# Weight sums of the recurrence stage: adding transfers in one spaced list that is held while a head is normalised, copies in 256 KB pieces on the load queue

## The chip, the cores and the metric

The kernel runs on one core of a Trainium2 chip. The metric is the device time of one execution in microseconds, the median of several runs; lower is better. The core has a matrix engine (TensorE, in the profile PE, with its weight loads as PEld), a vector engine (DVE), a scalar engine (ACT), GpSimd (POOL), and SyncE (SP), which only issues transfers. Each engine works through its own instructions in the order in which the program writes them, and waits where an instruction needs something that another engine or a transfer has yet to deliver. Transfers (DMAs) are issued by SP (the load queue, queue 1 in the profile) and by POOL (queue 0); both are carried out by the same 16 DMA engines.

## What is computed

A decoder of two layers works on 1024 tokens of width 1024 in float32. The first layer's token mixer is a gated linear recurrence with 8 heads, the second's a causal convolution module; each is followed by a squared-ReLU feed-forward part of width 4096, with normalisation after every part. What matters here is the first mixer, cut to its core:

```python
proj = h @ w_in                                   # q | forget | value | output gate
q = silu(q); f = lb + (1 - lb) * sigmoid(fz); k = 1 - f
o = chunkwise_gated_recurrence(q, k, v, cumsum(log f))          # per head
o = o * rsqrt(mean(o * o, axis=-1) + 1e-6) * norm_g             # per head
out = (o * silu(g)) @ w_out
...
ff = square(relu(x @ ffn_w1[i])) @ ffn_w2[i]      # i = 0, 1
```

The line with `rsqrt` is the normalisation of a head.

## The kernel before

All large products are in float32 accuracy: each operand is split into a high and a low part, and a product takes three matmuls. The products of 2x2 blocks are done with seven block products instead of eight (the forms 1, 2, 6, 5, 7, 3, 4 in `ORDER`), for which sums of weight blocks are needed. For `ffn_w2`, which is used from about 870 us on, these sums are not made on the compute engines. They are made by transfers from DRAM to DRAM in advance: `block_sums` (line 399) makes, for one of 16 blocks of `ffn_w2` (two layers by eight), four sums of 512 KB each in a DRAM tensor `sum_w`. For one block it issues:

- two copies of 1 MB each, `v[:, 0:2]` and `v[:, 2:4]` (lines 419 and 420),
- an adding transfer of 1 MB onto `v[:, 0:2]` (line 421), which needs the first copy,
- two adding transfers of 512 KB (line 423), `v[:, 2] += v[:, 1]` and `v[:, 3] += v[:, 2]`, each of which needs the one before.

Adding transfers can be issued by POOL alone. In the recurrence stage the copies go through POOL as well. Twelve of the sixteen blocks are summed in this stage, the other four later in the program, in other ways.

The recurrence stage (about 60 to 420 us) is written out by hand in order. Its outer loop goes over 12 `PAIRS` of weight columns (line 1007), and for each over the 7 forms. `pair_product` issues 12 matmuls of 512 columns for one form, in four slots of three; after each slot `slot` calls `tick` (line 390), which advances a counter and issues the jobs that `later(n, job)` has put off to this tick. So the tick is the unit in which the order of all engines is written. Ticks say nothing of when an instruction runs: an engine that waits for nothing runs ahead of the written order.

Between the products the heads' recurrences are advanced by `step`, one part of the generator `recurrence` (line 634) at a time. The last parts of a head are these: `outer`, then `attend` for the first half of the tokens and, one tick later, `settle(0)`; then `attend` for the second half and, one tick later, `settle(1)`. `settle` (line 731) has ACT square the head's output and sum it (line 735), POOL make the scale with a TENSOR_SCALAR (line 736) and a power of -1/2 (line 518, in `power_m_half`) on a tile `ss`, and ACT apply the scale to `o` (line 741, four ticks later). `give` (line 746) then has PE transpose `o`; ACT writes the result to `kt` (line 754), and SP stores it to DRAM as `od` (line 762).

POOL has hardly more to do in this stage than `settle`'s two instructions and the transfers of `block_sums`. `block_sums` is called after every sixth form, with `gap=12`: the first copy at once, the second 6 ticks later, the three adding transfers 12, 24 and 36 ticks after the call.

SP issues, in written order, the weight blocks `pr` (line 585, 256 KB, a new one as soon as a buffer of five is free), the heads' values `v` (line 632), the heads' stores `od` (line 762), their loads `u` (line 916) and the gated stores `zd` (line 924).

Of the kernel before, what the change touches and what calls it, by code (L numbers as in the profile page):

```python
# [12 lines left out]
ALU = mybir.AluOpType  # L13
PSUM = bass.MemoryType.PSUM

P = 128
# [18 lines left out]
NPAR = TAP + KB * TAPS  # L35

KBYTES = 220
PAIRS = [("q", 0), ("q", 1), ("q", 2), ("q", 3), ("g", 0), ("q", 4), ("q", 5), ("q", 6), ("g", 1), ("q", 7), ("g", 2), ("g", 3)]
NPOOL = (12, 11)
SEQ = "P00 P01 P02 P03 P04 P05 P06 P07 P10 P11 P12 P13 N0 P14 F0 P15 S0 P16 P17 UA0 UA1 E2 E3 N1 E4 F1 E5 E6 S1 E7 UB0 UB1 L2 L3 L4 L5 L6 L7"  # L40
# [4 lines left out]
ORDER = (1, 2, 6, 5, 7, 3, 4)  # L45
# [223 lines left out]
def body(ctx, tc, d, out):  # L269
    nc = tc.nc  # L270
    cst = ctx.enter_context(tc.tile_pool(name="cst", bufs=1))
    stat = ctx.enter_context(tc.tile_pool(name="stat", bufs=4))
    dram = ctx.enter_context(tc.tile_pool(name="dram", bufs=1, space=bass.MemoryType.DRAM))
    space = ctx.enter_context(tc.tile_pool(name="space", bufs=1)).ring(KBYTES * 1024)
    banks = ctx.enter_context(tc.tile_pool(name="ps", bufs=1, space=PSUM)).tile([P, 8, HT], F32, name="ps")
# [4 lines left out]
    def view(kb, shape, dt=F32, name="t"):  # L280
        at, top = int(kb * 1024), KBYTES * 1024
        if at < edge[0]:
            if edge[0] < top:
                space.tile([P, (top - edge[0]) // 4], F32, name="gap")
            edge[0] = 0
        if at > edge[0]:
            space.tile([P, (at - edge[0]) // 4], F32, name="gap")
        edge[0] = at + (prod(shape) + 7) // 8 * 32
        return space.tile([P, *shape], dt, name=name)
# [90 lines left out]
    vd = [[dram.tile([P, NTB, HT], F32, name=f"vd{m}{n}") for n in range(2)] for m in range(2)]  # L380

    ticks, waiting = [0], []

    def later(n, job):
        if n:
            waiting.append((ticks[0] + n, job))
        else:
            job()

    def tick(n=1):  # L390
        for _ in range(n):
            ticks[0] += 1
            for at, job in [w for w in waiting if w[0] <= ticks[0]]:
                waiting.remove((at, job))
                job()

    sums = {}

    def block_sums(name, layer, c, after=None, gap=0, adds=None):

        t = sums[name, layer, c] = dram.tile([4, P, 1024], F32, name=f"sum_{name}{layer}{c}")
        v, w = t.rearrange("a p n -> p a n"), d[name][layer, c].rearrange("a p n -> p a n")
        queue = nc.sync if after is not None else nc.gpsimd
        if adds is not None:

            def copies(rows, after):
                nc.sync.dma_start(out=t[0:4:2, rows.start, 0:1], in_=after)
                queue.dma_start(out=v[rows, 0:2], in_=w[rows, 0:4:2])
                queue.dma_start(out=v[rows, 2:4], in_=w[rows, 0:2])

            copies(slice(16, P), after)
            adds.append(lambda after: copies(slice(0, 16), after))
            adds.append(lambda after: nc.gpsimd.dma_start(out=v[:, 0:2], in_=w[:, 2:4], accum_op=ALU.add))
            for i in (2, 3):
                adds.append(lambda after, i=i: nc.gpsimd.dma_start(out=v[:, i], in_=v[:, i - 1], accum_op=ALU.add, max_dma_last_dim=4096))
            return
        if after is not None:
            nc.sync.dma_start(out=t[0:4:2, 0, 0:1], in_=after)
        queue.dma_start(out=v[:, 0:2], in_=w[:, 0:4:2])
        later(gap // 2, lambda: queue.dma_start(out=v[:, 2:4], in_=w[:, 0:2]))  # L420
        parts = [lambda: nc.gpsimd.dma_start(out=v[:, 0:2], in_=w[:, 2:4], accum_op=ALU.add)]
        for i in (2, 3):
            parts.append(lambda i=i: nc.gpsimd.dma_start(out=v[:, i], in_=v[:, i - 1], accum_op=ALU.add, max_dma_last_dim=4096))
        for i, part in enumerate(parts):
            later((i + 1) * gap, part)

    to_sum = [(*of, c) for of in (("w2", 0), ("w2", 1)) for c in range(NFC)]

# [72 lines left out]
    for k in range(4):  # L501
        c = slice((k % 2) * HT, (k % 2 + 1) * HT)
# [14 lines left out]
    def power_m_half(dst, src, n):  # L517
        nc.gpsimd.tensor_tensor(out=dst, in0=src, in1=nhalf[:, :n], op=ALU.pow)  # L518
# [61 lines left out]
    def load_block():  # L580
        p, b = divmod(at_block[0], 4)
        if p < len(PAIRS) and free:
            at_block[0] += 1
# [3 lines left out]
    def make_form(wait=1):  # L587
        p, i = divmod(at_form[0], 7)
        if p == len(PAIRS):
            return  # L590
# [30 lines left out]
    qk, gates, vts = {}, {}, {}  # L621
# [12 lines left out]
    def recurrence(h):  # L634
# [71 lines left out]
        for n in (32, 64):  # L706
            for s in range(0, n2, 2 * n):
                c, r = divmod(s, P)
# [22 lines left out]
        def settle(half):  # L731
            ss = stat.tile([P, 2, 4], F32, tag="ss", name="ss")
            cs = range(half * NTB, half * NTB + NTB)
            for c in cs:
                nc.scalar.activation(o[:, c], out_ps[:, c, :], AF.Square, scale=1.0 / QSCALE, accum_out=ss[:, 0, c % NTB : c % NTB + 1])
            nc.gpsimd.tensor_scalar(out=ss[:, 1], in0=ss[:, 0], scalar1=1.0 / P, scalar2=RMS_EPS, op0=ALU.mult, op1=ALU.add)
            power_m_half(ss[:, 0], ss[:, 1], 4)

            def rest():
                for c in cs:  # L740
                    nc.scalar.activation(o[:, c], out_ps[:, c, :], AF.Copy, scale=ss[:, 0, c % NTB : c % NTB + 1])
                later(1, lambda: ready.add(half))

            later(4, rest)
# [22 lines left out]
        def values(c):  # L767
            return vts[2 * h + c // NTB][:, c % NTB]

        def outer(cs):  # L770
            for c in cs:
                tensor.matmul(state_ps[:, c % NTB], kt[:, c, :], values(c), start=True, stop=True)

        def chain(cs):
            for c in cs:
                new = p1("state")
                if c == 0:
                    vector.tensor_copy(out=new, in_=state_ps[:, 0])
                else:
                    vector.scalar_tensor_tensor(out=new, in0=states[c], scalar=dec[:, c : c + 1], in1=state_ps[:, c % NTB], op0=ALU.mult, op1=ALU.add)  # L780
                states.append(new)

        def attend(cs):
            for c in cs:
                tensor.matmul(out_ps[:, c, :], A[:, c, :], values(c), start=True, stop=c == 0)
                if c:
                    tensor.matmul(out_ps[:, c, :], Q[:, c * P : (c + 1) * P], states[c], start=False, stop=True)

        outer(range(NTB))
        later(1, lambda: chain(range(NTB)))  # L790
        yield
# [2 lines left out]
        later(1, lambda: (chain(range(NTB, nk)), settle(0)))  # L794
        yield
        attend(range(NTB, 2 * NTB))
        later(1, lambda: settle(1))
        if h < H - 2:
            for half in range(2):
                load_values(2 * h + 2 + half)  # L800
# [23 lines left out]
    def evacuate(p, i, st, ps):  # L824
        kind, j = PAIRS[p]
        m, n = {2: (0, 0), 7: (1, 1), 3: (0, 1)}.get(i, (1, 0))
# [44 lines left out]
    def pair_product(p, i, f, st):  # L871
        ps = banks[:, st["banks"]["a" if i == 2 else "b" if i in (5, 3) else "z"]]
        for k in range(4):
# [5 lines left out]
            if k == 3:  # L879
                later(1 if p == len(PAIRS) - 1 and i in (3, 4) else 3, lambda: evacuate(p, i, st, ps))  # L880
            slot()
# [20 lines left out]
    def slot():  # L902
        tick()
        gate_turn()
        pace[0] += pace[1]
        if pace[0] >= 1:
            pace[0] = pace[0] - 1 if step() else 0.0

    to_load, loaded, to_gate = [], [], []
# [73 lines left out]
    for _ in range(5):  # L983
# [5 lines left out]
    p1 = Room(  # L989
        ((144, 152), (164, 172), (136, 144), (172, KBYTES)),  # L990
        {
# [14 lines left out]
    tick(4)  # L1006
    for p, (kind, j) in enumerate(PAIRS):
        st = {"banks": dict(turn_of)}
        turn_of = {"z": turn_of["a"], "a": turn_of["b"], "b": turn_of["z"]}
        pace[1] = 0.0 if p == 0 else 0.6 if p < 3 else 0.5  # L1010
        if kind == "g" and p < len(PAIRS) - 1:
            to_load += [(2 * j, 0), (2 * j + 1, 1), (2 * j, 1), (2 * j + 1, 0)]
        if p == len(PAIRS) - 1:
            seam()
        for i in ORDER:
            if kind == "q" and i == 2:
                while any(a[0] <= j - 3 for a in active) or recs and recs[0] <= j - 3:
                    tick()
                    step()
            pair_product(p, i, made.pop(0), st)  # L1020
            later(2, make_form)
            if (7 * p + ORDER.index(i)) % 6 == 1 and len(to_sum) > 4:
                block_sums(*to_sum.pop(0), gap=12)
        if kind == "q":
            later(4, lambda j=j: recs.append(j))
    early_out = ((0, 0), (1, 0), (2, 0))
# [7 lines left out]
    while step():  # L1034
        tick()
    tick(100)
    assert not waiting and not loaded and not to_load and not gates, (waiting, gates)
    order.close()
    oT = [o[0] for o in oT]

# [145 lines left out]
    class Up:  # L1186
# [14 lines left out]
        def settle(self, c):  # L1201

            for q in range(2):
                self.first(self.of[c], q)
# [415 lines left out]
    rest, adds = [None, None], []  # L1620
# [303 lines left out]
```

## Time and profile before

| | |
|---|---|
| Median of 3 runs | 2055.2 us (2055.06 to 2062.24) |
| Span of the profiled execution | 2068.3 us (the profile gives no other time of it) |
| PE busy | 2031.0 us, 98% |
| DVE, ACT, POOL busy | 1482.9, 1090.2 and 388.4 us |
| Load queue (queue 1) | 456.93 MB, 62.6% of the 16 engines' span |
| POOL's queue (queue 0) | 58.72 MB, 12.3% |
| Recurrence stage, 60 to 420 us | PE busy 344.72 of 360 us, DMA share 0.89 |

A row of the waits reads: engine, tile and line that waited, what it waited for, then total microseconds, times, and the longest. A row of the timeline reads: start and duration in microseconds, engine, line, operation, what it writes and reads, and in brackets the idle time of the engine before it with what ended that. Matmuls and small vector operations all bear line 204, the line of a helper, and are told apart by their tiles: `ps<-xf,fs` are the products of the recurrence stage, `ps<-ident,o` the transposes of a head's output, `ps` a bank of PE's accumulators, `fs` a weight form and `t` a product on its way to a gate. `sum_w<-in_w_dram` are the copies and the first adding transfer, `sum_w<-sum_w` the other two. POOL's DMA rows show the time for issuing, not for the transfer. A row of the windows gives the stretch and its length, the busy time (and count) of PE, PEld, DVE, ACT and POOL, the granted clock of PE, the DMA share and GB/s.

### The profile page before, as it was taken

Reading aid. Unit: us, or ns where it says so; the run is one execution under the profiler, and the core shown is the slowest. Engines: PE = TensorE matmul, PEld = TensorE weight load, DVE = VectorE, ACT = ScalarE, POOL = GpSimd, SP = SyncE. Lnnn points to the kernel's source line nnn. Section 1 sums busy time; section 2 is a strip of 40 time slices with the busy share of each in tenths; the row PEclk is TensorE's granted clock in tenths of the full one; section 3 lists DMA queues with packets and bytes.
Section 4 is the critical chain, followed back from the end, with each engine's and each line's share of the span. In section 5 each row is a group of like instructions: output and inputs, shape, how many; then the busy total and the mean of one; then the engine's idle time right before and its main releaser. Section 6 shows DMA issues by size and latency. Waiting matters only on the chain. (4 is left out here: it accounts for less than half of the span.)

```text
span 2068.3 us, 29719 instructions
## 1 busy us (share of the span) xinstructions
PE 2031.0 (98%) x11192; PEld 1674.5 (81%) x11192; DVE 1482.9 (72%) x1976; ACT 1090.2 (53%) x1727; POOL 388.4 (19%) x387
## 2 busy tenths in 40 slices
PE   8999999999999999999999999999999999999998
PEld 7888777788888888888888888888878878888886
DVE  8698877877775666565567898889589666755556
ACT  5456555641464555444444776488625555343333
POOL 0112222111001000000001699079210000100002
PEclk9999999999999999999999999999999999999999
DMA  4778889852689786999998855587759778996542
GB/s 186 224 195 233 238 224 270 254 189 81 187 288 298 243 295 221 353 341 332 335 349 292 309 193 185 190 323 271 256 215 339 245 232 291 386 292 204 193 155 102
DMA packets 183944, 517.55 MB, mean 250 GB/s; under 512 B 17912, under 2 KB 49784, under 8 KB 182776
## 3 DMA queue, kind: packets, MB, share of 16 engines
q1 hardware_dynamic: 168312, 456.93, 62.6%
q0 software_dynamic: 15488, 58.72, 12.3%
q8 instruction: 87, 1.43, 0.3%
q14 instruction: 57, 0.47, 0.1%
HBM read 380.85 MB, written 201.85 MB: 282 GB/s over the span
## 5 line engine op out<-in xcount | busy, mean ns | idle before, releaser
L204 PE MATMUL ps<-dw,dh 128*128 128x512 f32 x2688 | 611.6, 389 | 1.9 <-ACT dh L72 1.1
L204 PEld LDWEIGHTS ps<-dw,dh 128*128 128x128 f32 x2688 | 504.1, 188 | 107.2 <-ACT dh L72 1.6
L204 PE MATMUL ps<-x1f,fw 128*128 128x512 f32 x1344 | 309.3, 390 | 2.3 <-DVE c L204 1.2
L204 PEld LDWEIGHTS ps<-x1f,fw 128*128 128x128 f32 x1344 | 251.1, 188 | 56.2 <-ACT c L1224 2.3
L204 PE MATMUL ps<-xf,fs 128*128 128x512 f32 x1008 | 249.3, 398 | 4.1 <-issue 1.9
L204 POOL TENSOR_TENSOR cb<-cb,prod 128x512 f32<-128x512 f32 x168 | 222.7, 1334 | 12.9 <-ACT prod L1555 2.3
L204 DVE TENSOR_TENSOR dh<-dh 128x1024 fp32r<-128x1024 f32 x112 | 136.4, 1222 | 117.3 <-ACT dh L72 117.1
L204 PEld LDWEIGHTS ps<-xf,fs 128*128 128x128 f32 x1008 | 184.5, 189 | 43.4 <-issue 2.1
L204 DVE SCALAR_TENSOR_TENSOR ps<-u,par,ps 128x512 f32<-128x512 f32 x296 | 206.2, 750 | 11.0 <-ACT ps L1567 9.5
L72 ACT CAST dh<-dh 128x1024 fp32r<-128x1024 f32 x112 | 117.4, 1051 | 163.7 <-DMA dh<-hf 163.7
L204 PE MATMUL ps<-xa,wa 128*128 128x512 f32 x864 | 203.1, 392 | 0.1
L204 PEld LDWEIGHTS ps<-xa,wa 128*128 128x128 f32 x864 | 160.3, 188 | 33.3 <-ACT ha L1289 0.3
L204 DVE TENSOR_TENSOR dw<-dr,dw 128x1024 fp32r<-128x1024 f32 x112 | 136.2, 1222 | 66.6 <-ACT dw L72 65.9
L72 ACT CAST dw<-dr 128x1024 fp32r<-128x1024 f32 x112 | 117.0, 1051 | 119.2 <-PE ps L204 100.2
L1555 ACT ACTIVATE prod<-u,par 128x512 f32<-128x512 f32 x168 | 119.8, 726 | 36.6 <-POOL cb L204 35.7
L518 POOL TENSOR_TENSOR mv<-mv,nhalf 128x1 f32<-128x1 f32 x32 | 43.3, 1355 | 407.6 <-DVE mv L204 407.6
L1408 POOL COPY next<-ss 128x1 f32<-128x1 f32 x38 | 21.2, 558 | 413.8 <-DVE spare L204 265.1
L204 PE MATMUL ps<-xb,wa 128*128 128x512 f32 x384 | 91.1, 393 | 0.0
L204 PE MATMUL ps<-w,oT 128*128 128x512 f32 x384 | 89.5, 391 | 1.3 <-ACT oT L932 0.8
L204 DVE TENSOR_TENSOR spare<-next,spare 128x1024 fp32r<-128x1024 f32 x38 | 46.5, 1224 | 60.6 <-ACT spare L1401 60.5
L204 PE MATMUL ps<-vw,xf 128*128 128x512 f32 x336 | 79.8, 399 | 6.0 <-ACT vw L435 5.2
L204 PEld LDWEIGHTS ps<-w,oT 128*128 128x128 f32 x384 | 71.5, 188 | 16.6 <-ACT oT L932 1.2
(236 smaller groups left out, 2959.6 us busy)
## 6 DMA issues: line engine op xcount, KB each, us to landing
wa<-ready SPq DMA_DIRECT2D x140, 512.0 KB, 5.5
dh<-hf SPq DMA_DIRECT2D x112, 512.0 KB, 5.3
sum_w<-in_w_dram POOLq DMA_DIRECT2D x40, 1024.0 KB, 10.9
ready<-spare SPq DMA_DIRECT2D x76, 512.0 KB, 4.6
raw<-in_w1q_dram SPq DMA_DIRECT2D x66, 512.0 KB, 4.4
dr<-sum_w SPq DMA_DIRECT2D x64, 512.0 KB, 5.7
hf<-ht SPq DMA_DIRECT2D x112, 256.0 KB, 4.9
dr<-in_w_dram SPq DMA_DIRECT2D x48, 512.0 KB, 5.3
```

The lines of the kernel that those rows point to most:

```text
L72: self.nc.scalar.copy(out=slot[:, 0, c], in_=raw[:, c])
L204: return op(*args, **kw)
L518: nc.gpsimd.tensor_tensor(out=dst, in0=src, in1=nhalf[:, :n], op=ALU.pow)
L1408: nc.gpsimd.tensor_copy(out=raw[:, :1], in_=now)
L1555: nc.scalar.activation(tp, u[:, k : k + HT], AF.Copy, scale=tap(j, k))
```

## The change

The two copies are no longer issued by POOL but by SP, each in four pieces of 32 of the 128 rows (256 KB), one piece in every second tick from the first tick after the call: eight pieces within 15 ticks. The three adding transfers of a block are put into one list, `adding`. At every tick `add_some` looks through the list in order and issues at most one transfer: the next of a block whose time has come. The first is due 20 ticks after the call, the others 16 ticks (`SPACE`) after their predecessor was issued, and between any two there are at least 4 ticks. No adding transfer is issued while `quiet` is not zero, that is from a head's `outer` until its `settle(1)` has been issued. `block_sums` is called after every fifth form instead of every sixth, again for twelve blocks. The other calls of `block_sums` issue what they did.

```diff
+SPACE = 16
...
+    adding, quiet, added = [], [0], [0]
...
             for at, job in [w for w in waiting if w[0] <= ticks[0]]:
                 waiting.remove((at, job))
                 job()
+            add_some()
+
+    def add_some():
+        for one in adding:
+            if not quiet[0] and one[0] <= ticks[0] and added[0] <= ticks[0]:
+                one.pop(1)()
+                one[0], added[0] = ticks[0] + SPACE, ticks[0] + SPACE // 4
+                if len(one) == 1:
+                    adding.remove(one)
+                break
...
-        queue.dma_start(out=v[:, 0:2], in_=w[:, 0:4:2])
-        later(gap // 2, lambda: queue.dma_start(out=v[:, 2:4], in_=w[:, 0:2]))
-        parts = [lambda: nc.gpsimd.dma_start(out=v[:, 0:2], in_=w[:, 2:4], accum_op=ALU.add)]
+
+        def copies():
+            queue.dma_start(out=v[:, 0:2], in_=w[:, 0:4:2])
+            queue.dma_start(out=v[:, 2:4], in_=w[:, 0:2])
+
+        parts = [copies, lambda: nc.gpsimd.dma_start(out=v[:, 0:2], in_=w[:, 2:4], accum_op=ALU.add)]
         for i in (2, 3):
             parts.append(lambda i=i: nc.gpsimd.dma_start(out=v[:, i], in_=v[:, i - 1], accum_op=ALU.add, max_dma_last_dim=4096))
-        for i, part in enumerate(parts):
-            later((i + 1) * gap, part)
+        if turns:
+
+            def piece(to, src, r):
+                later(2 * (r // 32) + 8 * (to // 2) + 1, lambda: nc.sync.dma_start(out=v[r : r + 32, to : to + 2], in_=src[r : r + 32]))
+
+            for to, src in ((0, w[:, 0:4:2]), (2, w[:, 0:2])):
+                for r in range(0, P, 32):
+                    piece(to, src, r)
+            adding.append([ticks[0] + SPACE + 4, *parts[1:]])
+        else:
+            for part in parts:
+                part()
...
+        quiet[0] += 1
         outer(range(NTB))
...
         attend(range(NTB, 2 * NTB))
-        later(1, lambda: settle(1))
+        later(1, lambda: (settle(1), quiet.append(quiet.pop() - 1)))
...
-            if (7 * p + ORDER.index(i)) % 6 == 1 and len(to_sum) > 4:
-                block_sums(*to_sum.pop(0), gap=12)
+            if (7 * p + ORDER.index(i)) % 5 == 1 and len(to_sum) > 4:
+                block_sums(*to_sum.pop(0), turns=True)
```

More of the change, by code (lines that the diff above doesn't have):

```diff
@@ L395, in tick, with block_sums @@
                 job()
+            add_some()
[7 more added lines that the diff above has]
+                break
     sums = {}
[L399 removed]
+    def block_sums(name, layer, c, after=None, turns=False, adds=None):
         t = sums[name, layer, c] = dram.tile([4, P, 1024], F32, name=f"sum_{name}{layer}{c}")
@@ L1036, in body @@
     tick(100)
-    assert not waiting and not loaded and not to_load and not gates, (waiting, gates)
+    assert not waiting and not loaded and not to_load and not gates and not adding, (waiting, gates, adding)
     order.close()
```

## The prediction

> **What bounds the kernel now.** I read the page first, then the waits and the windows of the stretch in which the change works, then the timeline around the three longest gaps of PE there.
>
> ```profile
> span 2068.3 us, 29719 instructions
> PE 2031.0 (98%) x11192; PEld 1674.5 (81%) x11192; DVE 1482.9 (72%) x1976; ACT 1090.2 (53%) x1727; POOL 388.4 (19%) x387
> q1 hardware_dynamic: 168312, 456.93, 62.6%
> q0 software_dynamic: 15488, 58.72, 12.3%
> ```
>
> PE is the bound: 2031.0 of 2068.3 us. So a microsecond counts only if PE stood still in it, and all that PE's idle time holds is 37.3 us. The page gives no time of the profiled execution beside its span, which is 13.1 us (0.6%) above the median of the three runs, 2055.2. I work out a difference in the profiled execution and take it off the median. About 0.5% of the time, 10.3 us, is what a measurement of this kernel can tell from no change.
>
> The change works only in the recurrence stage, roughly 60 to 420 us.
>
> ```profile
> 60.00:420.00 360.00, 344.72 (x3614) 285.12 (x3613) 282.94 (x458) 206.04 (x474) 76.35 (x92) 0.99 0.89 240
> 268.50:273.30 4.80, 0.00 (x0) 0.00 (x0) 0.00 (x0) 1.19 (x5) 2.44 (x3) 0.93 1.06 218
> 272.60:276.00 3.40, 2.70 (x128) 2.37 (x132) 1.63 (x4) 3.37 (x9) 0.00 (x0) 0.50 1.04 183
> 392.10:395.40 3.30, 3.30 (x132) 2.96 (x132) 2.38 (x4) 2.93 (x11) 2.03 (x3) 0.50 0.64 195
> ```
>
> The first number after the stretch's length is PE's busy time; the last three are granted clock, DMA share and GB/s. PE idles 15.3 us here (360 less 344.72), more than a third of all its idle time. The DMA engines are 0.89 busy. And the granted clock is 0.50 in two stretches of about 3.4 us.
>
> ```profile
> POOL sum_w L423 <- DMA sum_w<-in_w_dram: 110.6, 12, 11.9
> POOL sum_w L421 <- issue: 45.1, 7, 7.1
> ACT o L741 <- POOL ss L518: 20.2, 9, 6.1
> PE ps L204 <- ACT o L741: 7.8, 4, 4.9
> PE ps L204 <- issue: 1.9, 1, 1.9
> ```
>
> Read from the top, this is one chain: POOL waits for the landing of one adding transfer before it may issue the next (total, times, longest), ACT waits for POOL's two small instructions that give a head its scale, PE waits for ACT. The timeline shows the chain closing:
>
> ```profile
> 269.47 1.22 POOL L421 DMA_DIRECT2D sum_w<-in_w_dram  x1 [6.23 <-issue]
> 270.77 0.19 POOL L736 TENSOR_SCALAR ss<-ss 128x4 f32<-128x4 f32 x1
> 271.04 1.03 POOL L518 TENSOR_TENSOR ss<-ss,nhalf 128x4 f32<-128x4 f32 x1
> 272.11 1.14 ACT L741 ACTIVATE o<-ps,ss 128x128 f32<-128x128 f32 x4 [6.09 <-POOL ss L518]
> 273.30 1.12 PE L204 MATMUL ps<-ident,o 128*128 128x128 f32 x4 [4.86 <-ACT o L741]
> ...
> 382.27 0.22 ACT L735 ACTIVATION_READ_ACCUMULATOR o<-ps 128x1 f32 x1
> 388.04 0.86 POOL L423 DMA_DIRECT2D sum_w<-sum_w  x1 [11.37 <-DMA sum_w<-in_w_dram]
> 388.98 0.19 POOL L736 TENSOR_SCALAR ss<-ss 128x4 f32<-128x4 f32 x1
> 391.50 0.66 PE L204 MATMUL ps<-ident,o 128*128 128x128 f32 x4 [2.27 <-ACT o L741]
> ...
> 352.19 1.14 ACT L741 ACTIVATE o<-ps,ss 128x128 f32<-128x128 f32 x4 [3.16 <-POOL ss L518]
> 353.40 1.09 PE L204 MATMUL ps<-xf,fs 128*128 128x512 f32 x4 [1.86 <-issue]
> ```
>
> ACT had the last square sum of a head at 382.49; POOL took it up at 388.98, because L423 stood before it in POOL's order and waited 11.37 us for a landing. L736 shows no wait of its own in these two places: its input had long been there. At 353.40 the profile names no releaser, but the ACT row just above it is late by the same cause, so I count that gap too.
>
> **The change part by part.** *The copies leave POOL.* 24 transfers of 1 MB, two a block, become 96 of 256 KB on the load queue, eight a block, one in every second tick. POOL is rid of 24 issues of about 1 us; the rows of the two lines are alike, and this is one:
>
> ```profile
> L420 POOL DMA_DIRECT2D sum_w<-in_w_dram x12 | 11.6, 970 | 0.0
> ```
>
> SP gets 96 issues; a load of the same size takes it 0.33 us (row at 314.41, below), so 32 us in all on an engine that mostly waits; PE does not see them.
>
> The moved bytes stay. Queue 1 takes 62.6% of 2068.3 us for 456.93 MB, 2.83 us of all 16 engines a MB; queue 0 4.33. Queue 0's 58.72 MB are 25.2 MB of copies (12 blocks of 2.1) and 33.5 MB of adding (16 blocks). With the copies at queue 1's price (71 us of queue 0's 254), adding costs 5.5 us a MB. A block thus costs 5.9 us of copies and 11.4 us of adding, 208 us for the twelve, before and after.
>
> *The spacing and the hold.* To see what stands before a head's scale on POOL afterwards I counted ticks along the written program.
>
> ```profile
> 153.04 0.19 POOL L736 TENSOR_SCALAR ss<-ss 128x4 f32<-128x4 f32 x1 [11.99 <-ACT o L735]
> ...
> 417.18 0.19 POOL L736 TENSOR_SCALAR ss<-ss 128x4 f32<-128x4 f32 x1 [22.49 <-ACT o L735]
> sum_w<-in_w_dram POOLq DMA_DIRECT2D x40, 1024.0 KB, 10.9
> sum_w<-sum_w POOLq DMA_DIRECT2D x32, 512.0 KB, 8.2
> ```
>
> The first and the last head's first L736 stand at ticks 182 and 431, so a tick is 264.1/249 = 1.06 us. The holds are ticks 177-185, 210-219, 246-255, 282-291, 326-335, 362-371, 398-407 and 428-433. A block starts every 20 ticks from tick 108 to 330; with the rules of 20, 16 and 4 ticks and the holds, the 36 adding transfers go out from tick 128 to 392, always in an order in which a block's next step comes at least 16 ticks, 17 us, after its last one. They land in 10.9 and 8.2 us. The tightest places are the second head's end (tick 246, its predecessor at 230, the head's L736 at 251) and two like it; there a landing has 21 ticks, 22 us. So no head's scale should stand behind a waiting DMA, and POOL will run ahead of the written order instead. The last adding transfer falls at tick 392, some 375 us, against 393.81 us for the last one before: the load per microsecond stays near the present 0.89, since the holds give back what the closer start of the blocks takes.
>
> *The sum.* Removed: 4.86 and 2.27 us of PE's wait for ACT o (the other two of the four, 0.7 us together, I leave, since one of them has POOL waiting for ACT), 1.86 us at 353.40, and half of the two stretches at clock 0.50, as each follows one of the first two gaps: 0.5 x (3.4 + 3.3) = 3.4 us. Together 12.4 us. DVE stood still in the longest gap as well (0.00 in its row), so it has no backlog that would take the place of the wait.
>
> The half clock is weighed once more against a page: the Trainium skill, "TensorE: Matmul & The Clock Gate", Part 1, says that PE's clock falls to half after at least one idle window of about 3.4 us. The gap of 4.86 us agrees with it; the one of 2.27 us is shorter than that and was followed by 0.50 all the same, so the measurement decides. By the page alone only one stretch would go, and the sum would be 10.7 us.
>
> Added: the copies now stand ahead of loads and stores in one queue. What a late transfer of that queue costs is seen once:
>
> ```profile
> 314.41 0.33 SPq L585 DMA_DIRECT2D pr<-in_wp_dram  x1
> 319.95 2.01 SPq L762 DMA_DIRECT2D od<-kt  x1
> 326.47 0.69 DVE L204 TENSOR_TENSOR total<-pr 128x512 f32<-128x512 f32 x1 [0.62 <-DMA pr<-in_wp_dram]
> 334.71 0.48 ACT L724 COPY kt<-ps 128x384 f32<-128x384 f32 x1 [1.46 <-DMA od<-kt]
> 337.64 2.56 PE L204 MATMUL ps<-xf,fs 128*128 128x512 f32 x10 [1.45 <-ACT t L837]
> pr<-in_wp_dram SPq DMA_DIRECT2D x48, 256.0 KB, 7.0
> ```
>
> A weight block issued at 314.41 was needed 0.62 us before 326.47, 11.4 us after its issue, and came late by those 0.62 us; a head's store issued at 319.95 held ACT 1.46 us and, through it, PE 1.45 us. Bounds: from -1.45 us (the stores leave earlier where POOL is no longer late, and this one wait goes too) to 8 x 1.45 = 11.6 us (every head pays it). I take 3 us, two more such waits, being nearest to the row: one in eight now, and the queue's mean load does not grow. Net 12.4 - 3 = 9.4 us: 2055.2 - 9.4 = 2045.8, say 2046.
>
> **The rivals.** *A, the whole gain:* nothing is paid on the load queue and the wait at 337.64 goes as well: 12.4 + 1.5 = 13.9 us, 2041. For it speaks that loads have slack now: over the whole stage DVE's only wait for a weight block was that 0.62 us. Against it, DMA at 0.89.
>
> *B, the gain is eaten:* heads wait no more, but stores and weight blocks come late by 1.45 us at each of seven more heads, 10.2 us: 2055.2 - 12.4 + 10.2 = 2053.
>
> *C, slower:* the load queue becomes the wait. SP works in order, and what it may not yet issue piles up:
>
> ```profile
> 258.73 4.10 SPq L632 DMA_DIRECT2D v<-vd  x2
> 273.86 0.33 SPq L762 DMA_DIRECT2D od<-kt  x1
> ```
>
> It stood still for some 11 us here, five pieces' worth of ticks. Freed, it would issue those at once: five pieces of 0.26 MB at 2.83 us are 3.7 us, and 7.4 if queue 0 takes every other turn, all ahead of the next weight block. That block was needed 11.4 us after its issue, and the median landing is 7.0; with 7.4 more it comes 3.0 us late, and DVE, then ACT and PE stand behind it. For the eleven later weight groups that is 33 us: 2055.2 - 12.4 + 33 = 2076. It decides from a queue of 4.4 us ahead of each block. Against it: the pieces are two ticks apart, SP's stall there was itself due to the late scale, and PE has four weight forms made ahead. The Trainium skill, "DMA: Bandwidth & Descriptors", Queues, rings and completion order, says that an engine consumes one queue's descriptors in ring order; no run here shows it, and it is this rival's rule.
>
> *D, the change does not do what it says:* the adding transfers land later than 22 us after issue, and heads wait as now: 2055. The median of 10.9 us speaks against it.
>
> **How the numbers follow.** The forecast (2042 to 2050) has 0.52, A (2036 to 2042) 0.16, B 0.15, C 0.12, D 0.05. The range from 2039 to 2058 leaves out C and the lower part of A, together under 0.2. Faster by over 0.5% means under 2044.9: all of A and just under half of the forecast, 0.40. Slower by over 0.5% means over 2065.5: C, 0.12. The rest, 0.48, is within. The likeliest case's own range stands above.
>
> **What would show it.** In the profile after, POOL's L736 should follow ACT's last square within 2 us at every head, and the row of ACT o waiting for POOL ss fall from 20.2 to under 5 us. PE's wait for ACT o should fall from 7.8 to about 1, and the granted clock be 1.00 through the stage. PE should be idle 5 to 7 us less between 60 and 420. The DMA share should stay near 0.89, the median landing of weight blocks rise from 7.0 to 8 or 9, and waits of ACT and DVE for od, zd, u or pr stay under 5 us. I am wrong if those waits are 10 us or more (B, C), if POOL's DMA issues still stand waiting before L736 (D), or if PE idles as long for a releaser not named here.

## The result, and the profile after

The changed kernel takes 2068.9 us (median of six runs, 2067.1 to 2074.4) against 2056.5 us for the kernel before (six runs, 2055.1 to 2062.2). The ratio is 1.0054, with a 95% interval from 1.0039 to 1.0069: the change makes the kernel slower by about 11 us, where 9.4 us of gain were forecast.

The page of the changed kernel, the same lines as were shown of before:

```profile
span 2067.5 us, 29823 instructions
PE 2030.6 (98%) x11192; PEld 1676.7 (81%) x11192; DVE 1483.8 (72%) x1976; ACT 1092.4 (53%) x1727; POOL 367.4 (18%) x363
q1 hardware_dynamic: 175992, 482.11, 65.1%
q0 software_dynamic: 8960, 33.56, 8.6%
```

The work is the same. The copies have moved from queue 0 to queue 1, and what is left in queue 0, 33.56 MB of adding, takes 8.6% of 2067.5 us: 5.3 us a MB, near the 5.5 worked out beforehand. This profiled execution took 2069.3 us, 1.8 over its span. So the profiled execution of before, with its span of 2068.3 us, took some 2070 us, more than any of the six timed runs of that kernel. I therefore profiled the kernel before a second time (first experiment, span 2056.0 us, time 2058.0) and compare with that one. Over the 107 times of this kernel beside the experiments the median is 2060.0 us and the longest 2067.9, ten of them over 2065: the first profile stands at the end of a spread, the second a little under its middle. The windows of the stage, first of this second profile of before, then of the changed kernel:

```profile
60.00:420.00 360.00, 349.49 (x3647) 288.95 (x3646) 288.92 (x466) 214.44 (x496) 79.71 (x94) 1.00 0.90 248
210.00:330.00 120.00, 116.71 (x1311) 97.18 (x1310) 99.41 (x164) 74.05 (x178) 30.86 (x36) 1.00 0.93 249
330.00:390.00 60.00, 55.90 (x657) 46.90 (x656) 51.28 (x86) 34.95 (x94) 14.90 (x17) 1.00 0.91 234
```

```profile
60.00:420.00 360.00, 343.91 (x3595) 284.95 (x3594) 281.65 (x456) 206.84 (x472) 57.90 (x68) 0.99 0.85 238
210.00:330.00 120.00, 114.46 (x1289) 95.43 (x1290) 95.92 (x158) 72.26 (x174) 26.05 (x29) 0.99 1.04 284
330.00:390.00 60.00, 53.89 (x509) 45.33 (x508) 47.25 (x78) 31.85 (x78) 8.82 (x11) 0.94 0.66 172
227.40:230.70 3.30, 3.30 (x14) 3.01 (x13) 3.27 (x5) 1.65 (x9) 1.30 (x2) 0.50 1.01 277
343.40:350.20 6.80, 5.75 (x15) 4.59 (x16) 5.07 (x9) 2.03 (x4) 0.00 (x0) 0.50 0.75 217
```

PE idles 360 - 343.91 = 16.1 us in the stage instead of 10.5, which is 5.6 us. In the two stretches at clock 0.50 PE was busy for 3.30 + 5.75 us; I estimate their cost at half of that, 4.5 us. Together 10.1 us, most of the 11.5 us between the two spans. The DMA share was nearly even before (0.93, then 0.91); now it is 1.04 for 120 us and then 0.66.

The waits of the changed kernel in the stage:

```profile
ACT kt L749 <- DMA od<-kt: 12.3, 4, 7.0
PE ps L205 <- DVE state L205: 6.6, 2, 4.3
PE ps L205 <- ACT t L863: 6.1, 1, 6.1
ACT o L766 <- POOL ss L543: 4.5, 5, 1.4
DVE t L205 <- DMA u<-od: 3.2, 2, 3.0
PE ps L205 <- ACT kt L749: 1.1, 1, 1.1
PE ps L205 <- ACT o L766: 0.4, 1, 0.4
```

The wait that the change was to remove is gone: ACT o waits 4.5 us for POOL ss, never over 1.4, and PE 0.4 us for ACT o. In its place ACT waits 12.3 us for heads' stores `od`, since a head's `kt` may not be overwritten before it is stored. The timeline shows the longest of these (rows in between are left out):

```profile
320.03 0.69 ACT L779 ACTIVATE kt<-ps,nrm 128x512 f32<-128x512 f32 x1 [1.51 <-PE ps L205]
324.10 3.76 SPq L442 DMA_DIRECT2D sum_w<-in_w_dram  x2
329.57 0.33 SPq L787 DMA_DIRECT2D od<-kt  x1
342.48 0.48 ACT L749 COPY kt<-ps 128x384 f32<-128x384 f32 x1 [7.01 <-DMA od<-kt]
343.81 0.59 ACT L863 COPY t<-ps 128x512 f32<-128x512 f32 x1
344.45 1.65 PE L205 MATMUL ps<-xf,fs 128*128 128x512 f32 x3 [6.11 <-ACT t L863]
```

The head's second half was ready at 320.72. SP issued its store only at 329.57, after two pieces of a copy, and it landed some 12.9 us later, at about 342.4. ACT stood 7.01 us before `kt`, the copy to `t` behind it came late, PE stood 6.11 us, and the clock was halved from 343.4 to 350.2. The other long gap of PE, 4.3 us for DVE's `state` at 226.38, has another source: DVE had stood 3.0 us for a load `u<-od`. SP's waits in the stage show why it was late in issuing; the three longest rows of them that name a landing:

```profile
SPq L442 <- DMA sum_w<-in_w_dram: 16.5, 14, 1.9
SPq L442 <- DMA pr<-in_wp_dram: 13.2, 8, 2.8
SPq L610 <- DMA sum_w<-in_w_dram: 9.9, 7, 2.6
```

In these rows a piece or a weight block is held until an earlier transfer has landed with which it shares no data. All rows of SP that name a landing, those with shared data among them (a load `u` waits for its store `od`), make 65 us in the changed kernel and 13 us in the kernel before.

### The profile page after: what moved, and what is told of

The parts are those of the page before. It is cut to its first block, busy times and chain, and to the rows that moved or that the text cites. A ratio compares the mean times of both kernels' runs of the same rounds, so it can differ in the third digit from the quotient of the medians.

```text
span 2067.5 us, 29823 instructions
## 1 busy us (share of the span) xinstructions
PE 2030.6 (98%) x11192; PEld 1676.7 (81%) x11192; DVE 1483.8 (72%) x1976; ACT 1092.4 (53%) x1727; POOL 367.4 (18%) x363
## 3 DMA queue, kind: packets, MB, share of 16 engines
q1 hardware_dynamic: 175992, 482.11, 65.1%
q0 software_dynamic: 8960, 33.56, 8.6%
## 4 chain that ended last, share of the span: by engine, by line
PE 69%; DMA 14%; DVE 8%; ACT 4%; issue 4%; POOL 1%; SPq 1%; DVEq 0%; ACTq 0%; POOLq 0%
PE ps L205 69%; DMA sum_w<-in_w_dram 2%; DMA next<-in_wpw_dram 2%; DMA raw<-in_w1q_dram 1%; DMA od<-kt 1%; DMA hf<-ht 1%; DMA dh<-hf 1%; DVE fw L205 1%; DMA dr<-in_w_dram 1%; DMA hf<-hr 1%; POOL cb L205 1%; DMA vr<-in_wv_dram 1%; ACT hr L1225 1%; DMA pr<-in_wp_dram 1%; ACT c L1224 1%
## 5 line engine op out<-in xcount | busy, mean ns | idle before, releaser
L205 POOL TENSOR_TENSOR cb<-cb,prod 128x512 f32<-128x512 f32 x168 | 223.1, 1337 | 12.5 <-ACT prod L1581 2.0
L1434 POOL COPY next<-ss 128x1 f32<-128x1 f32 x38 | 19.2, 506 | 414.7 <-DVE spare L205 266.4
```

The source lines that it names most:

```text
L205: return op(*args, **kw)
L1434: nc.gpsimd.tensor_copy(out=raw[:, :1], in_=now)
```

## The experiments

Ratios are to the kernel before, timed beside it on the same chip. For every kernel the table gives four sums of the stage: PE's idle time (360 us less its busy time from 60 to 420), POOL's waits for landings before adding and copying transfers, SP's waits for landings before an issue, and ACT's wait before it may overwrite `kt` (each the sum of the waits' rows from 60 to 430 us that name a DMA), all in us.

| kernel | ratio (95%) | PE idle | POOL | SP | ACT kt |
|---|---|---|---|---|---|
| before, second profile (e1) | | 10.5 | 162 | 13 | 0 |
| the change | 1.0054 (1.0039 to 1.0069) | 16.1 | 113 | 65 | 12.3 |
| e2 no sums in the stage | 0.9968 (0.9954 to 0.9982) | 6.3 | 0 | 4 | 0 |
| e3 list, copies on POOL | 1.0012 (0.9999 to 1.0024) | 13.1 | 22 | 13 | 1.7 |
| e4 pieces, old times | 1.0008 (0.9996 to 1.0021) | 11.3 | 217 | 20 | 0 |
| e5 od stores by ACT | 1.0049 (1.0034 to 1.0064) | 16.9 | 132 | 72 | 0 |
| e6 pieces by ACT | 1.0064 (1.0047 to 1.0081) | 17.6 | 110 | 91 | 7.8 |
| e7 every sixth product | 1.0044 (1.0029 to 1.0059) | 15.3 | 138 | 52 | 10.6 |
| e8 no hold | 1.0035 (1.0019 to 1.0051) | 13.2 | 147 | 71 | 8.5 |
| e9 before, fewer blocks here | 0.9971 (0.9963 to 0.9980) | 6.2 | 145 | 13 | 0 |
| e10 list, one block at a time | 1.0012 (1.0002 to 1.0022) | 13.5 | 202 | 28 | 2.7 |
| e11 the change, no adds here | 0.9971 (0.9960 to 0.9982) | 5.8 | 0 | 4 | 0 |
| e12 the change, fewer blocks | 0.9985 (0.9971 to 0.9999) | 8.7 | 108 | 25 | 3.1 |
| e13 the change, 1 MB copies | 1.0067 (1.0050 to 1.0085) | 22.3 | 107 | 21 | 13.6 |
| e14 e4 with 128 KB pieces | 1.0031 (1.0018 to 1.0044) | 13.8 | 231 | 57 | 0 |
| e15 e12 with 1 MB copies | 0.9981 (0.9970 to 0.9991) | 7.6 | 107 | 17 | 5.4 |
| e16 e13, od stores by ACT | 1.0061 (1.0045 to 1.0077) | 19.6 | 94 | 15 | 0 |
| e17 e13, copies by ACT | 1.0063 (1.0041 to 1.0084) | 18.0 | 90 | 35 | 4.9 |

**What could be gained.** e1 is the kernel before with no edit.

> The kernel before, once more, for a second profile. Theory 1 (the moved copies make the heads' stores on the load queue land late; and the gaps of 4.86 and 2.27 us that the prediction took away belong to the one profiled execution of before, whose span was 13 us over the median): time 2055 to 2060 us, the two gaps on ACT o gone or under 2 us together, at most one stretch at half clock in the stage. If the first profile was typical (theory 2, the new order of the adding transfers is at fault): span near 2068 us or the same gaps of about 7 us in a shorter run.

The waits of this second profile of before:

```profile
ACT o L741 <- POOL ss L518: 12.2, 8, 3.2
PE ps L204 <- ACT o L741: 3.1, 3, 1.8
PE ps L204 <- issue: 1.7, 1, 1.7
```

PE's wait for ACT o was 7.8 us in the first profile and is 3.1 here, with none over 1.8, and the clock in the stage is 1.00. The two long gaps and the two half-clock stretches on which the forecast stood are not there. How often other executions have them, two profiles don't say.

e2 leaves the sums out of the stage; later products read a plain weight block in place of each sum (that part of the edit isn't printed).

```
             if (7 * p + ORDER.index(i)) % 6 == 1 and len(to_sum) > 4:
-                block_sums(*to_sum.pop(0), gap=12)
+                to_sum.pop(0)
```

> The kernel before with the twelve block sums of the recurrence stage left out (the later products read weight blocks in place of the sums, same bytes): the ceiling of what any order of these transfers can bring. Theory 1: under 10 us faster than before (2047 to 2054 us), since before's typical run loses little to them. Theory 2, with the first profile typical: 13 us or more faster (2043 us or less).

```profile
60.00:420.00 360.00, 353.69 (x3669) 293.03 (x3668) 291.82 (x470) 217.17 (x500) 24.46 (x34) 1.00 0.35 114
```

With no copies and no adding here at all, the DMA share falls from 0.90 to 0.35, and the kernel is 0.32% faster, 6.6 us. No ordering of these transfers can gain much more than that; 9.4 us were not there.

**The two parts apart.** e3 has the list, the hold and the new pace, with the copies on POOL as before; e4 has the pieces on the load queue, with the adding transfers at their old times (and the old pace, every sixth product).

```
-            for to, src in ((0, w[:, 0:4:2]), (2, w[:, 0:2])):
-                for r in range(0, P, 32):
-                    piece(to, src, r)
+            queue.dma_start(out=v[:, 0:2], in_=w[:, 0:4:2])
+            later(6, lambda: queue.dma_start(out=v[:, 2:4], in_=w[:, 0:2]))
```

```
-            adding.append([ticks[0] + SPACE + 4, *parts[1:]])
+            for i, part in enumerate(parts[1:]):
+                later((i + 1) * 12, part)
...
-        quiet[0] += 1
...
-        later(1, lambda: (settle(1), quiet.append(quiet.pop() - 1)))
+        later(1, lambda: settle(1))
...
-            if (7 * p + ORDER.index(i)) % 5 == 1 and len(to_sum) > 4:
+            if (7 * p + ORDER.index(i)) % 6 == 1 and len(to_sum) > 4:
```

> The kernel after with the copies put back on POOL, whole, as before (the first at the call, the second 6 ticks later): list, spacing, hold and the call after every fifth form stay. Theory 1: as fast as before within 5 us (2052 to 2060 us), ACT's wait for od under 3 us. Theory 2: still slow, 2064 us or more.

> The other part alone: copies in 256 KB pieces on the load queue, but adding transfers 12, 24 and 36 ticks after the call, no list and no hold, the call after every sixth form. Theory 1: slow as after, 2064 us or more, ACT waits 8 us or more for od stores. Theory 2: as before, 2054 to 2060 us.

Neither part alone costs what both cost: 1.0012 and 1.0008, and both intervals reach 1. For e4 the expectation that the pieces alone would delay the stores missed; ACT never waited for one. e3 has two waits for stores:

```profile
ACT t L859 <- DMA zd<-t: 4.2, 1, 4.2
ACT kt L745 <- DMA od<-kt: 1.7, 1, 1.7
```

e11 is the change with its adding transfers left out of the stage, so that these sums stay unadded.

```
-            adding.append([ticks[0] + SPACE + 4, *parts[1:]])
```

> The kernel after with the adding transfers of these twelve blocks left out (the sums stay unadded), so that the load queue carries the same pieces at the same ticks and POOL's queue nothing. Theories B and F: no od wait above 1 us, 2050 to 2056 us, near the kernel with no sums. Theory Q (the pieces ahead of the stores in one queue suffice): od waits of 5 us or more remain, 2062 us or more.

0.9971, as fast as with no sums at all (e2). Pieces that stand in the load queue between loads and stores cost nothing while no adding transfers run beside them; the DMA share of the stage is 0.56 then.

**Queue order, or the number of transfers?** In e5 the stores are issued by ACT, in e6 the pieces.

```
-                nc.sync.dma_start(out=od[h][half], in_=on[:, part])
+                nc.scalar.dma_start(out=od[h][half], in_=on[:, part])
```

```
-                later(2 * (r // 32) + 8 * (to // 2) + 1, lambda: nc.sync.dma_start(out=v[r : r + 32, to : to + 2], in_=src[r : r + 32]))
+                later(2 * (r // 32) + 8 * (to // 2) + 1, lambda: nc.scalar.dma_start(out=v[r : r + 32, to : to + 2], in_=src[r : r + 32]))
```

> The kernel after with the heads' stores od issued from ACT, so that they go through another queue than the copies' pieces. Theory Q (the stores are late because they stand in one queue behind the pieces): ACT's wait for od falls from 12.3 us to under 3, time 2054 to 2061 us. Theory B (they are late because the 16 DMA engines are full of pieces and adding transfers at that time, whatever the queue): the wait stays at 8 us or more and the time over 2064 us.

> The kernel after with the 96 pieces issued from ACT in place of SP. ACT pays for 96 issues, some 30 us in small bits. Theory Q: waits for od, zd and pr all fall under 3 us together; PE's gaps for them go; time 2055 to 2063 us with ACT's own cost. Theory B: waits for od and zd stay at 8 us or more, over 2066 us.

Neither helps. The timeline of e5 shows that the same wait came along to ACT (rows left out at the dots):

```profile
321.62 0.69 ACT L779 ACTIVATE kt<-ps,nrm 128x512 f32<-128x512 f32 x1 [1.54 <-PE ps L205]
...
330.97 0.33 ACTq L787 DMA_DIRECT2D od<-kt  x1
331.34 1.65 ACT L690 COPY at<-blocks 32x256 f32<-32x256 f32 x4 [8.03 <-DMA sum_w<-in_w_dram]
```

The store's data were ready at 322.31. ACT stood idle for 8.03 us and issued the store at the end of that time; the row behind the issue names as releaser the landing of a transfer of weights into a sum, which the copy in that row doesn't use. So I read the wait as one of issuing, which comes along to another engine. The pieces in e6 met it too, for 12.5 us at one place. Neither run can therefore tell what the order in the queue alone is worth. That made a third theory: the small pieces bring too many transfers under way at once. e13 keeps the bytes and has a quarter of the transfers; e14 is e4 with twice as many, one of 128 KB in every tick.

```
-                later(2 * (r // 32) + 8 * (to // 2) + 1, lambda: nc.sync.dma_start(out=v[r : r + 32, to : to + 2], in_=src[r : r + 32]))
+                later(8 * (to // 2) + 1, lambda: nc.sync.dma_start(out=v[:, to : to + 2], in_=src))
```

```
-                later(2 * (r // 32) + 8 * (to // 2) + 1, lambda: nc.sync.dma_start(out=v[r : r + 32, to : to + 2], in_=src[r : r + 32]))
+                later(r // 16 + 8 * (to // 2) + 1, lambda: nc.sync.dma_start(out=v[r : r + 16, to : to + 2], in_=src[r : r + 16]))
```

> The change with each copy as one 1 MB transfer on the load queue, in place of four of 256 KB: the same bytes, 24 transfers for 96. Theory N (number in flight: an issue waits for the landing of an earlier transfer once too many are under way, and the small pieces are what fills that number): SyncE's waits for landings between 60 and 430 us fall from 65 to under 25 us, ScalarE's wait for od from 12.3 to under 4, ratio 0.999 to 1.002. Theory S (share: copies and adds of several blocks at once fill the 16 engines, whatever the number of transfers): DMA share 1.0 or more in 210 to 330 and the wait for od still over 8 us, ratio 1.003 to 1.007.

> The pieces on the load queue with the adding transfers at their old times, but of 128 KB, one in every tick: 192 transfers in place of 96, the same bytes at the same pace. Theory N: SyncE's waits for landings rise from 20.5 to 50 us or more, ScalarE waits for od again, ratio 1.003 or more (with 256 KB it was 1.0008). Theory S: as with 256 KB, 0.9996 to 1.002.

Windows and waits of e13:

```profile
210.00:330.00 120.00, 114.80 (x1289) 95.82 (x1289) 95.06 (x157) 71.61 (x174) 26.39 (x30) 0.97 1.02 277
```

```profile
ACT kt L748 <- DMA od<-kt: 13.6, 3, 6.6
PE ps L205 <- DVE state L205: 10.8, 3, 6.4
PE ps L205 <- ACT t L862: 6.9, 1, 6.9
```

SP's waits for landings fell from 65 to 21 us, as theory N said, and the kernel is no faster: 1.0067. So the number is not the main cause. It is not free either: in e14 SP waits 57 us where e4 has 20, and 1.0031 stands against 1.0008 (intervals that barely touch), though ACT waits for no store in either. e16 and e17 put the question of order once more, now with few transfers: the stores by ACT in the one, the copies by ACT in the other.

```
-                nc.sync.dma_start(out=od[h][half], in_=on[:, part])
+                nc.scalar.dma_start(out=od[h][half], in_=on[:, part])
```

```
-                later(8 * (to // 2) + 1, lambda: nc.sync.dma_start(out=v[:, to : to + 2], in_=src))
+                later(8 * (to // 2) + 1, lambda: nc.scalar.dma_start(out=v[:, to : to + 2], in_=src))
```

> e13's kernel (1 MB copies on the load queue) with the heads' stores od issued by ScalarE in place of SyncE, so that they stand behind no copy in the load queue. With 256 KB pieces the same edit could not tell, since ScalarE's own issue then waited 8.0 us for a landing. Theory R (order: stores stand behind copies in one queue, which drains slowly while the adding transfers run): od lands in under 8 us, ScalarE's wait for od falls from 13.6 to under 4, ratio 1.004 or less. Theory S (share: the 16 engines are full, whatever the queue): od lands late and ScalarE waits for it as before, 8 us or more, ratio 1.0045 to 1.008.

> e13's kernel with the 24 copies of 1 MB issued by ScalarE in place of SyncE: no load and no store stands behind a copy. Theory R: SyncE's issues take 0.33 us again (3.65 and 2.67 at 321.65 and 325.40 in e13), ScalarE's wait for od is under 4 us, ratio 1.003 or less. Theory S: DMA share 1.0 or more in 210 to 330, ScalarE's wait for od 8 us or more, ratio 1.0045 to 1.008. About 24 issues of 0.7 us on ScalarE cost little under either: ScalarE is busy 53%.

1.0061 and 1.0063. In e16 ACT no longer waits before `kt`, but once more it stood before issuing a store, for 11.6 us:

```profile
ACT at L689 <- DMA v<-vd: 11.6, 1, 11.6
```

So e16 tells as little of order as e5. What speaks against theory R is e17: there no load or store stands behind a copy, and weight blocks and stores are late all the same. A weight block landed as late as 19.2 us after its issue (15.3 at most in e1 and in the changed kernel). Theory S's own signs, a share of 1.0 and 8 us of waiting for `od`, didn't come either (0.98 and 4.9). Two rows of e17's waits:

```profile
DVE total L205 <- DMA pr<-in_wp_dram: 7.3, 2, 6.8
ACT kt L748 <- DMA od<-kt: 4.9, 1, 4.9
```

**The pace, the hold, the turns.** e7 starts blocks at the old pace, e8 drops the hold (the `quiet` lines, as in e4), and e10 has the old pace and lets the list serve one block at a time, 7 ticks apart.

```
-            if (7 * p + ORDER.index(i)) % 5 == 1 and len(to_sum) > 4:
+            if (7 * p + ORDER.index(i)) % 6 == 1 and len(to_sum) > 4:
```

```
-        for one in adding:
+        for one in adding[:1]:
...
-                one[0], added[0] = ticks[0] + SPACE, ticks[0] + SPACE // 4
+                one[0], added[0] = ticks[0] + 7, ticks[0] + 7
```

> The kernel after with the call after every sixth form, as before, in place of every fifth. Theory B or density: a sixth less load per microsecond, od waits fall to under 5 us, time 2056 to 2063 us. Theory Q alone: the pieces stand as close within their block as in after, so od waits stay at 8 us or more, over 2064 us. Theory R (the release of the hold issues several adding transfers at once, just ahead of the stores): as after, since the hold stays.

> The kernel after without the hold; list, spacing and pieces stay. Theory R: the od waits fall from 12.3 to under 4 us, the time to 2055 to 2062 us, although POOL's scale may be late again by some us. Theories Q and B: the od waits stay at 8 us or more, over 2064 us.

> The kernel after with the adding transfers of one block at a time (the list's first block alone may issue, 7 ticks apart) and the call after every sixth form; pieces on the load queue and the hold stay. Theory F (pieces and the adding transfers of two or three blocks are in flight together and make the heads' stores late): od waits under 3 us, DMA share under 1.00 in 210 to 330 us, time 2054 to 2062 us. If the pieces or the hold alone do it: as every_sixth, 2066 us or more.

Slower blocks alone do not cure it (1.0044), nor does dropping the hold (1.0035). Serving one block at a time takes most of it away (1.0012). e7 and e10 have the same pieces, pace and hold and differ only in the list: blocks in turns with 16 and 4 ticks between transfers in e7, one block at a time with 7 in e10. Turns and spacing aren't told apart. First the waits of e7, then of e10:

```profile
POOL sum_w L438 <- DMA sum_w<-in_w_dram: 68.8, 8, 11.6
ACT kt L749 <- DMA od<-kt: 10.6, 3, 4.4
```

```profile
POOL sum_w L438 <- DMA sum_w<-in_w_dram: 88.9, 9, 14.3
POOL sum_w L438 <- DMA sum_w<-sum_w: 58.4, 8, 9.3
ACT kt L749 <- DMA od<-kt: 2.7, 1, 2.7
```

In e10 POOL waits 202 us in all before adding transfers, in e7 138. With one block at a time the block's next adding transfer can't go before its last one has landed; with several blocks in turns there is more often one whose last step has landed, and POOL issues sooner. How full the engines are doesn't sort these kernels: between 210 and 330 us the DMA share is 0.94 in e7 (1.0044), 0.96 in e10 (1.0012) and 0.98 in e4 (1.0008). Down the table, among the kernels that have twelve blocks' copies off POOL's queue and their adds in the stage, the ratio follows that column: 217 and 202 us of POOL's waiting go with 1.0008 and 1.0012, 147 to 110 with 1.0035 to 1.0064, 107 to 90 with 1.0061 to 1.0067. e14, with its doubled number, is the one outside the row. This order was read off after the runs, so it supports the reading and doesn't prove it.

**Where the load has room.** e9 is the kernel before with 8 blocks in the recurrence instead of 12, and 6 in the feed-forward stage instead of 2; e12 and e15 are the change with the same split.

```
-            if (7 * p + ORDER.index(i)) % 6 == 1 and len(to_sum) > 4:
+            if (7 * p + ORDER.index(i)) % 9 == 1 and len(to_sum) > 8:
...
-        if c in (0, 2):
+        if c < 6:
```

> The kernel before with 8 instead of 12 block sums in the recurrence stage (every ninth form in place of every sixth) and 6 instead of 2 in the feed-forward stage after it, where the DMA share is 0.66. Same transfers in sum, same order within a block. Theory B (the stage pays for how full the 16 engines are): DMA share in the stage about 0.7, PE's gaps there shrink towards those without any sums, 3 to 6 us faster than before. If the full engines do not matter in before: within 2 us of before.

> The change on top of e9: list, spacing, hold and pieces as in after, but 8 blocks in the recurrence stage (every ninth form) and 6 in the stage after it. If the change's own steps cost only where the 16 engines are full: od waits under 1 us, the stage as clean as in e9, 2052 to 2057 us and within 2 us of e9. If pieces, list or hold cost by themselves: 2059 us or more.

> The change with 1 MB copies on the load queue, and with eight blocks in the recurrence and six in the stage after it, as in the version that beat both kernels (0.9971). Theory N: nothing is left that waits, SyncE's waits for landings under 20 us, ratio 0.996 to 0.9985. Theory S: the same, since the share is near 0.74; this run only asks whether the change is worth anything where there is room. If ScalarE waits 3 us for od as with 256 KB pieces (0.9985), the small price there was not the number of pieces.

Windows of e9, the recurrence and the stage that takes the load:

```profile
60.00:420.00 360.00, 353.83 (x3670) 293.16 (x3670) 291.95 (x470) 217.42 (x500) 59.84 (x74) 1.00 0.74 208
430.00:800.00 370.00, 369.12 (x1686) 306.46 (x1685) 252.27 (x322) 175.71 (x260) 35.75 (x39) 1.00 0.81 263
```

At a share of 0.74 PE idles 6.2 us, as little as with no sums at all, and POOL's old way costs nothing: 2054.5 us against 2059.6. This version beats both kernels, by 0.29% and, through the ratios, some 0.8%. The change on top of it (e12, 0.9985; e15, 0.9981) gains nothing more; its ratios lie a little behind e9's, and the intervals overlap. ACT still waits 3.1 and 5.4 us for stores there, with small pieces and with large; for e12 under 1 us was expected.

## Why the prediction was wrong

**The added term, 3 us, is the step that failed.** It said that the load queue would bring two more waits like the row of 1.46 us, since "the queue's mean load does not grow". By the two profiles PE idles 5.6 us more although 4.4 us of old waits are gone (next paragraph), so the new idle time is 10.0 us, and 4.5 us of half clock come on top: some 14.5 us, more than even its bound of 11.6 us. The kind of wait was right: a late store holds `kt`, then ACT, then PE, and rival B named late stores. But ACT's four waits are 3.85, 0.58, 0.89 and 7.01 us, not 1.46, PE's longest gaps are 6.1 us behind the last of these and 4.3 us behind a late load `u`, and the added term held no half clock at all: the prediction had counted that on the side of the gain only. A sign that it named, weight blocks landing in 8 or 9 us at the median, didn't come (6.0): it was single transfers that were late.

**The removed term, 12.4 us, was mis-sized.** Its sizes came from one execution that stood 13.1 us over the median; the prediction named that distance and then took differences "in the profiled execution" off the median. In the second profile PE's waits for ACT o and at issue are 3.1 and 1.7 us and no stretch has half clock. By that profile what the change took away is 3.1 + 1.7 us less the 0.4 left, 4.4 us. e2 sets the end at 6.6 us.

**"The load per microsecond stays near the present 0.89" held only as a mean.** It compared one number, the last adding transfer, and that came early itself: 369.19 us, not 375. It left the copies out, which end far earlier now. The last copy of the kernel before, in its first profile's timeline:

```profile
362.60 1.06 POOL L420 DMA_DIRECT2D sum_w<-in_w_dram  x1
```

In the changed kernel the last two pieces go out from 324.10 to 327.86. The share over the whole stage stayed (0.90 and 0.85), but as 1.04 and then 0.66. A stage's mean hid it. This was not the main part of the loss, though: e7, with the old pace and shares of 0.94 and 0.85, still stands at 1.0044.

**"POOL will run ahead of the written order instead" was taken for free.** The runs show that it is not, once the copies are off POOL's queue: e4 and e10, in which POOL waits 217 and 202 us for landings, lose little, e7 with the same pieces and pace stands at 1.0044 with 138 us, and without adding transfers (e11) nothing is lost. My reading is that POOL's waiting for one landing before the next issue, which delayed heads by a few microseconds, also held the adding transfers back in favour of loads and stores. The prediction asked what a freed SP would issue (rival C), yet not what a freed POOL would.

**A smaller miss:** issuing a piece took SP 0.56 us at the median, some 53 us for the 96, not 0.33 and 32 us. e11 shows that this alone costs nothing.

**Rival C** was right in sign, and 7 us too high, by another cause. Its rule was that of the Trainium skill, "DMA: Bandwidth & Descriptors", Queues, rings and completion order: descriptors of one queue go in ring order. No run here shows that order itself, and the loss doesn't hang on it: e11 has all the pieces in the queue and no loss, and e17 takes the copies to another engine's queue and keeps the loss. SP's queue does show the strain (65 us of waits, a store issued 8.9 us after its data); in e13 the waits fall to 21 us and the time doesn't follow.

**What held:** POOL's scale no longer makes ACT wait more than 1.4 us; the price of adding; and the condition for being wrong, waits for `od`, `zd`, `u` or `pr` of 10 us or more.

**What stays open.** e3 has the list and 1 MB copies at a share of 1.01 between 210 and 330 and loses almost nothing, though its POOL hardly waits (22 us); e13 and e17 differ from it in that the copies are on SP's or ACT's queue, so that copies and adding transfers can run as two separate streams. That loads lose their turn to two streams and not to one is my reading; no run tests it. Nor does the trace say why an issue waits for the landing of an earlier transfer that has other data.

## What to carry to other kernels

Before you size a gap, set the profiled execution against the timed median and, if it lies off, profile again; and leave the work out once, since that run caps every reordering of it. An engine that waits for its own transfers may also be their throttle: before removing the wait, list what will then be in flight together, in stretches and not as a mean over the stage. Where the engines are nine tenths full, moving load to a stage with room was worth more here than any order within the stage.

## What the runs showed of the hardware

A gap of PE of 2.65 us was followed by half clock. e3's timeline and windows:

```profile
236.40 4.60 PE L205 MATMUL ps<-xf,fs 128*128 128x512 f32 x12 [2.65 <-ACT t L859]
```

```profile
236.40:239.80 3.40, 3.40 (x8) 2.73 (x9) 1.42 (x4) 3.08 (x8) 0.00 (x0) 0.50 1.14 273
```

The Trainium skill, "TensorE: Matmul & The Clock Gate", Part 1, asks for at least one idle window of about 3.4 us; this gap is shorter, as the one of 2.27 us in the first profile of before was, so the measurements go against that as a lower limit. Nor is the length of the gap all that decides: after e7's gaps of 3.01 and 3.05 us (338.78 and 410.00 us) the clock stayed at 1.00, as it did after the second profile's gaps, none over 1.8 us. The stretch is about 3.4 us long, and 6.8 us after the gap of 6.11 us.

An adding transfer between DRAM tensors occupied the engines 5.3 us a MB, about twice the 2.8 us a MB of queue 1 (65.1% of 2067.5 us for 482.11 MB).

A store of 256 KB landed in 2.3 us (median of the stage) where the engines had little else (e2), in 7.8 us in the kernel before (e1) and in 8.8 us in the changed kernel.
